# The first half of an input projection by a seven-product scheme, ahead of two attentions

## Chip, cores and metric

One core of one Trainium2 chip runs one layer of an encoder in float32. The metric is device time in microseconds, the median of several runs. In the profile's names, PE is TensorE (matmuls), PEld its weight loads, DVE is VectorE, ACT is ScalarE, POOL is GpSimd and SP is SyncE, which here only issues transfers.

## What is computed

```python
h  = rms_norm(x, norm_mix)                # x: 2048 tokens x 1024 features
z  = h @ w_in                             # 1024 x 4352
q_a, k_a, v_a, q_b, k_b, v_b, g_a, g_b = split(z, [512,128,128,512,512,512,1024,1024])
y_a = windowed_gqa(q_a, k_a, v_a, sink)   # 8 heads of 64, 2 K/V heads, |t-s| <= 128, ALiBi, sink
y_b = neighborhood_attn(q_b, k_b, v_b, rpb)  # 8 heads, 32 x 64 grid, 8 x 16 neighbours, learned bias
merged = sigmoid(g_a + b) * (y_a @ w_proj_a) + sigmoid(g_b + b) * (y_b @ w_proj_b)
x = x + merged @ w_out
x = x + relu(rms_norm(x, norm_mlp) @ w_up)**2 @ w_down
out = rms_norm(x, norm_final)
```

## The kernel before

Every float32 operand of a matmul is split into a high part (rounded) and a low part (the rest), and one product takes three matmuls: high by high, high by low, low by high (`mm3`, lines 187 to 189; `mm3s`, lines 735 to 737). `split_weights` and `split` make the parts: ACT casts, then POOL or DVE subtracts.

The layer runs in stages that follow each other in the program; a scheduler orders the instructions of each engine and may mix neighbouring stages.

1. **Start.** `make_h` loads four token tiles of 128 x 1024, normalises them, turns them with 32 transposes and writes `hT` pages (high and low) for one block of 512 tokens; four blocks in all. K and V of attention A and the first tile of Q (`first`) are projected along with it.
2. **Attention A.** 32 units (`attn_a`: 2 groups of heads x 16 blocks of 128 queries), each with scores, softmax, transposes and PV. Between them stand `dense` pieces: one piece is one tile of 128 columns of `w_in` times one block of 512 tokens, 24 matmuls (`feature_tile`). `paced` lets each piece go only after a given unit is done. There are 40 such pieces in this stage.
3. **V of attention B**, by tokens: `hT` is the stationary operand and 512 columns of weights move, 16 x 24 matmuls. Then the gate columns of token block 0, 16 pieces (`gate_tile`).
4. **Attention B.** 32 units (`attn_b`: 8 heads x 4 column groups), filled with the gate pieces of blocks 1 to 3: 48 pieces, five of them kept for after the last unit. Each head needs three bias tiles (`make_bias_b`: three loads, then POOL adds a mask), in two buffers.
5. **Projections, gates and `w_out`**, then the **up projection** and the **down projection**. Both of these use a scheme of seven block products for a 2 x 2 block product (Strassen's, in Winograd's form): sums of blocks of the weights (`up_left`) and of the tokens (`up_right`) are multiplied, and sums of products give the result (`up_quad`).

Q, K, V and the gates go to DRAM after the projection and are loaded again by the attentions. Buffers come from pools: a load into a buffer waits until the last reader of its tile before is done, and a pool on the left or right side of SBUF can be given up as a whole, whereupon the next pool lies in its place. Loads are issued by SP in order, most stores by ACT (`put`, `flush`).

Of the kernel before, what the change touches and what calls it, by code (L numbers as in the profile page):

```python
# [90 lines left out]
def encoder_layer(ctx, tc, x, norm_mix, w_in, b_gate, sink, rpb, w_pa, w_pb, w_out,  # L91
# [11 lines left out]

    cp = pool("cp", side="left")
    s_w = ExitStack()
    wp = pool("wp", side="right", stack=s_w)
    dp = pool("dp", space=DRAM)
    s_pp = ExitStack()
    pps = {t: pool(f"pp_{t}", space=PSUM, stack=s_pp) for t in ("mm", "s", "pt", "av")}

    n_ps = [0]

# [6 lines left out]
    def T(pl, shape, dt, tag, bufs):  # L119
        n_t[0] += 1  # L120
        return pl.tile(shape, dt, tag=tag, bufs=bufs, name=f"{tag}_{n_t[0]}")
# [23 lines left out]
    qs_a = [dp.tile([2, P, S], F32, name=f"qs_a{t}") for t in range(4)]  # L145
    qs_b = [dp.tile([2, P, S], F32, name=f"qs_b{t}") for t in range(4)]
    ks_a = dp.tile([2, P, S], F32, name="ks_a")
    ks_b = [dp.tile([2, P, S], F32, name=f"ks_b{t}") for t in range(4)]
    vs_a = dp.tile([S, 2, P], F32, name="vs_a")
    vs_b = dp.tile([S, BH, P], F32, name="vs_b")  # L150
# [21 lines left out]
    def slice_of(parts, pl=wp):  # L172

        raw = T(wp, [P, KC, P], F32, "raw", 2)
# [4 lines left out]
        hl = T(pl, [P, 2, KC, P], F32R, "whl", 2 if pl is wp else 1)  # L179
        split_weights(raw, hl)  # L180
        return hl
# [23 lines left out]
    def rstd_of(pl, t):  # L205

        st = T(pl, [P, 4], F32, "st", 4)
        junk = T(pl, [P, 512], F32, "junk", 1)
        for n in range(2):
            A.activation(junk, t[:, n * 512 : (n + 1) * 512], AF.Square, accum_out=st[:, n : n + 1])  # L210
# [5 lines left out]
    def normalised(pl, tiles):  # L216

        for t in tiles:
            V.tensor_scalar(t, t, rstd_of(pl, t), float(D) ** 0.5, ALU.mult, ALU.mult)

    def transposed(tiles, gain, pages, banks):

        hi, lo = pages
        for k in range(KC):
            ps = psum(*banks[k % len(banks)])
            for t in range(4):
                PE.transpose(ps[:, t * P : (t + 1) * P], tiles[t][:, k * P : (k + 1) * P], ident)
            h, l = hi[k // 4][:, k % 4, :], lo[k // 4][:, k % 4, :]
            A.activation(h, ps, AF.Copy, scale=gain[:, k : k + 1])  # L229
            V.scalar_tensor_tensor(out=l, in0=ps, scalar=gain[:, k : k + 1], in1=h.bitcast(F32),  # L230
                                   op0=ALU.mult, op1=ALU.subtract)

    def pages_of(pl, tag, bufs):
        return ([T(pl, [P, 4, BT], F32R, tag, bufs) for _ in range(2)],
                [T(pl, [P, 4, BT], F32R, tag, bufs) for _ in range(2)])


    s_h1 = ExitStack()
    s_h0 = ExitStack()
    s_x = ExitStack()  # L240
    h1 = pool("h1", side="left", stack=s_h1)
    h0 = pool("h0", side="left", stack=s_h0)
    xp = pool("xp", side="left", stack=s_x)
    xf = x[0]
    hp = []

    def make_h(b):
        pg = pages_of(h1 if b else h0, "hT", 12 if b else 4)
        tiles = [load_tile(xp, "xin", 8, xf[b * BT + t * P : b * BT + (t + 1) * P]) for t in range(4)]
        if b == 0:  # L250
            with tc.issue_after(last_dma[0]), nc.allow_non_contiguous_dma(reason="small per-feature vectors"):
                SY.dma_start(g_mix, norm_mix[0].rearrange("(k p) -> p k", p=P))
                SY.dma_start(g_mlp, norm_mlp[0].rearrange("(k p) -> p k", p=P))
                SY.dma_start(bg, b_gate[0].rearrange("(k p) -> p k", p=P))
                SY.dma_start(sink_t, bcast(sink[0], AH))
        normalised(xp, tiles)
        transposed(tiles, g_mix, pg, (("pt", 2), ("s", 2), ("pt", 2), ("s", 2), ("av", 1)))
        hp.append(pg)


    def qk_tile(pl, col, dst, scale, tiled=False, whl=wp):
        hl = slice_of([(cols(w_in[0], col), KC)], whl)
        yield
        for b in range(NB):
            ps = psum("mm", 3)
            feature_tile(ps, hl, hp[b])
            th = T(wp, [P, BT], F32, "z", 2)
            tl = T(pl, [P, BT], F32, "el", 2)
            if tiled:

                pv = ps.rearrange("p (r j c) -> p j r c", r=8, j=4)
                hv, lv, hr, lr = (flipped(t) for t in (th, tl, th.bitcast(F32R), tl.bitcast(F32R)))
                A.copy(hr, pv)
                V.tensor_tensor(out=lr, in0=pv, in1=hv, op=ALU.subtract)
            else:
                A.activation(th.bitcast(F32R), ps, AF.Copy, scale=scale)
                V.scalar_tensor_tensor(out=tl.bitcast(F32R), in0=ps, scalar=scale, in1=th,
                                       op0=ALU.mult, op1=ALU.subtract)
            flush()
            for e in range(2):  # L280
                for z, t in enumerate((th, tl)):
                    put(dst[e, z * 64 : z * 64 + 64, b * BT : (b + 1) * BT], t[e * 64 : e * 64 + 64, :])
            yield

    def v_tile(pl, col, dst):
        hl = slice_of([(cols(w_in[0], col), KC)])
        yield
        for b in range(NB):
# [4 lines left out]
            p2 = psum("mm", 3)  # L293
            for t in range(4):
                PE.transpose(p2[:, t * P : (t + 1) * P], vt[:, t * P : (t + 1) * P], ident)
            flush()
            v2 = T(pl, [P, 4, 2, 2, 64], F32, "v2", 1)
            p2v = p2.rearrange("p (t e d) -> p t e d", t=4, e=2)
            A.copy(v2[:, :, :, 0].bitcast(F32R), p2v)
            V.tensor_tensor(out=v2[:, :, :, 1].bitcast(F32R), in0=p2v, in1=v2[:, :, :, 0], op=ALU.subtract)  # L300
            put(dst[b * BT : (b + 1) * BT].rearrange("(t p) e d -> p t (e d)", p=P),
                v2.rearrange("p t e z d -> p t (e z d)"))
            yield

    make_h(0)
    first = [qk_tile(xp, O_KA, ks_a, 1.0), v_tile(xp, O_VA, vs_a), qk_tile(xp, O_QA, qs_a[0], 0.125, whl=xp)]
    for f in first:
        next(f)
    for b in range(NB):
        if b + 1 < NB:  # L310
            make_h(b + 1)
        for f in first:
            next(f, None)
    for f in first:
        next(f, None)
    flush()
    s_x.close()


    s_a = ExitStack()  # L320
    ap_ = pool("ap", side="left", stack=s_a)
    rp = rpb[0]
    for n, (w, lo_rel) in enumerate(((24, -8), (32, -8), (24, -15))):
        tb = T(ap_, [BH, T_ROWS, w], F32, "v2", 1)
# [11 lines left out]
    def make_bias_a(g):  # L336
        t = T(ap_, [P, 4, 384], F32, "biasa", 1)
# [6 lines left out]
    def attn_a(g, i):  # L344
# [5 lines left out]
        for t in range(2):  # L350
            SY.dma_start(q[:, 2 * t : 2 * t + 2, :].bitcast(F32),
                         qs_a[2 * g + t][:, :, i * P : (i + 1) * P].rearrange("e p t -> p e t"))
        ka = T(ap_, [P, 2, 384], F32R, "ka", 2)
        SY.dma_start(ka[:, 0, lo:hi].bitcast(F32), ks_a[g, :, base + lo : base + hi])
        SY.dma_start(ka[0:64, 1, lo:hi].bitcast(F32), ks_a[g, 64:128, base + lo : base + hi])
        SY.dma_start(ka[64:128, 1, lo:hi].bitcast(F32), ks_a[g, 0:64, base + lo : base + hi])
        v = T(ap_, [P, 3, P], F32R, "va", 3)
        SY.dma_start(v[:, c0:c1, :].bitcast(F32),
                     vs_a[base + lo : base + hi, g, :].rearrange("(c p) d -> p c d", p=P))
# [66 lines left out]
    def units_a(g):  # L426
        make_bias_a(g)
        for i in range(16):
            yield attn_a(g, i)

    for _ in chain([qk_tile(ap_, O_QA + P, qs_a[1], 0.125)]):
        pass
    flush()
    dense = [qk_tile(ap_, O_QA + 2 * P, qs_a[2], 0.125), qk_tile(ap_, O_QA + 3 * P, qs_a[3], 0.125)]
    for t in range(4):
        dense.append(qk_tile(ap_, O_QB + t * P, qs_b[t], 1.0, tiled=True))
        dense.append(qk_tile(ap_, O_KB + t * P, ks_b[t], 0.125))
    fill = chain(dense)
    drive(units_a(0))
    paced(fill, range(8), 40, 0, 3)  # L440
    flush()
    drive(units_a(1))
    last_a = done[-1]
    paced(fill, range(8, 40), 40, 0, 3)
    del done[:]
    flush()
    s_a.close()

# [12 lines left out]
    gates_0 = chain(gate_tile(f, (0,)) for f in range(16))  # L461


    s_v = ExitStack()
    vp = pool("vp", side="left", stack=s_v)
    with tc.issue_after(last_a):
        for _ in range(4):
            next(gates_0)
    hl = T(vp, [P, 2, KC, BT], F32R, "whl", 1)
    for half in range(2):  # L470
        raw = T(vp, [P, 4, BT], F32, "raw", 2)
# [664 lines left out]
```

## Time and profile before

| what | value |
|---|---|
| runs | 2748.17, 2746.87, 2747.84 us, median 2747.84 |
| profiled execution | 2745.41 us, span 2743.6 us, granted TensorE clock 0.990 |
| busy | PE 2672.1 us (97%), DVE 1391.6 (51%), ACT 1181.5 (43%), POOL 808.5 (29%) |
| transfers | 482.73 MB, mean 176 GB/s |

The profile lists for a stretch of time the busy time of each engine with its number of instructions in brackets, then the granted TensorE clock, the share of time in which the 16 DMA engines were busy, and GB/s. In a list of instructions the columns are start, duration, engine and line, operation, tiles written and read, count, and in square brackets the idle time before and what ended it. Lines of a grouped list end in busy time, mean ns of one, and idle time before.

### The profile page before, as it was taken

The numbers are of one execution on the slowest core, as the hardware profiler recorded it, in microseconds if no ns is written. First come the engines' busy times: TensorE is split into PE (matmuls) and PEld (weight loads), VectorE is DVE, ScalarE is ACT, GpSimd is POOL, SyncE is SP. The second block draws the span as 40 slices with busy tenths as digits, with TensorE's granted clock in tenths as the row PEclk, the third lists the DMA queues.
The fourth block names the chain that finished last, engine by engine and source line by source line (L and its number), as shares of the span: only waits on it lengthen the run. The fifth ranks groups of instructions, "written<-read, shape, count | busy, mean of one in ns | idle before, by whom it ended". The sixth has DMA issues, their size and how long they took to land.

```text
span 2743.6 us, 35309 instructions
## 1 busy us (share of the span) xinstructions
PE 2672.1 (97%) x12472; PEld 2217.4 (81%) x12472; DVE 1391.6 (51%) x2174; ACT 1181.5 (43%) x2159; POOL 808.5 (29%) x614
## 2 busy tenths in 40 slices
PE   7999999999899999899999899989999999999998
PEld 6788888887788888787777688878887888888887
DVE  5155564000444443634436666586654644546666
ACT  7145454212454544533433444554444332322444
POOL 2122232213443441532431365556554000000000
PEclk9999999999999999999999999999999999999999
DMA  6556565436787785744645754474444954445555
GB/s 201 150 163 167 165 165 130 147 111 194 199 198 183 196 195 159 219 137 163 221 126 200 272 174 149 154 232 144 145 139 158 344 173 158 141 158 172 179 188 170
DMA packets 387584, 482.73 MB, mean 176 GB/s; under 512 B 32696, under 2 KB 237112, under 8 KB 386256
## 3 DMA queue, kind: packets, MB, share of 16 engines
q1 hardware_dynamic: 332816, 400.76, 47.7%
q10 hardware_dynamic: 54592, 79.72, 9.5%
q8 instruction: 99, 1.62, 0.3%
q14 instruction: 77, 0.63, 0.1%
HBM read 329.31 MB, written 151.06 MB: 175 GB/s over the span
## 4 chain that ended last, share of the span: by engine, by line
PE 84%; DMA 5%; DVE 5%; ACT 2%; issue 2%; POOL 1%; SPq 1%; ACTq 0%; POOLq 0%; DVEq 0%
PE b L735 14%; PE b L736 14%; PE b L737 14%; PE mm L189 9%; PE mm L188 9%; PE mm L187 9%; PE av L582 2%; PE pt L189 2%; DMA z<-zg 2%; PE pt L571 2%; PE pt L188 2%; PE pt L187 2%; PE s L545 2%; DVE ml L682 1%; PE pt L384 1%
## 5 line engine op out<-in xcount | busy, mean ns | idle before, releaser
L187 PE MATMUL mm<-hT,whl 128*128 128x512 f32 x960 | 383.9, 400 | 4.4 <-ACT hT L229 4.4
L188 PE MATMUL mm<-hT,whl 128*128 128x512 f32 x960 | 382.4, 399 | 0.0
L189 PE MATMUL mm<-hT,whl 128*128 128x512 f32 x960 | 380.9, 397 | 0.0
L736 PE MATMUL b<-dwh,dah 128*128 128x512 f32 x896 | 348.6, 389 | 0.0
L737 PE MATMUL b<-dwh,dah 128*128 128x512 f32 x896 | 346.4, 389 | 0.0
L735 PE MATMUL b<-dwh,dah 128*128 128x512 f32 x896 | 339.6, 389 | 2.7 <-ACT dah L731 2.7
L728 POOL TENSOR_TENSOR c<-c,c 128x512 f32<-128x512 f32 x120 | 233.6, 1961 | 229.6 <-issue 160.7
L170 POOL TENSOR_TENSOR whl<-raw,whl 128x1024 fp32r<-128x1024 f32 x80 | 199.6, 2498 | 299.6 <-ACT whl L169 292.6
L731 ACT CAST dah<-da 128x1024 fp32r<-128x1024 f32 (+1 forms) x128 | 120.8, 945 | 357.5 <-PE b L737 235.9
L732 DVE TENSOR_TENSOR dah<-da,dah 128x1024 fp32r<-128x1024 f32 (+1 forms) x128 | 139.3, 1090 | 226.0 <-ACT dah L731 225.9
L735 PE MATMUL b<-bh,whlb 128*128 128x512 f32 x592 | 232.0, 392 | 5.1 <-ACT whlb L731 2.7
L737 PE MATMUL b<-bh,whlb 128*128 128x512 f32 x592 | 231.0, 392 | 2.7 <-DVE whlb L732 2.6
L736 PE MATMUL b<-bh,whlb 128*128 128x512 f32 x592 | 231.4, 391 | 0.0
L187 PEld LDWEIGHTS mm<-hT,whl 128*128 128x128 f32 x960 | 181.5, 189 | 38.6 <-ACT hT L229 4.6
L188 PEld LDWEIGHTS mm<-hT,whl 128*128 128x128 f32 x960 | 181.8, 189 | 34.8
L189 PEld LDWEIGHTS mm<-hT,whl 128*128 128x128 f32 x960 | 181.4, 189 | 35.1
L735 PEld LDWEIGHTS b<-dwh,dah 128*128 128x128 f32 x896 | 168.2, 188 | 38.0 <-ACT dah L731 3.1
L728 DVE TENSOR_TENSOR c<-b,c 128x512 f32<-128x512 f32 x160 | 108.6, 688 | 177.6 <-PE b L737 171.0
L736 PEld LDWEIGHTS b<-dwh,dah 128*128 128x128 f32 x896 | 168.2, 188 | 34.9
L737 PEld LDWEIGHTS b<-dwh,dah 128*128 128x128 f32 x896 | 168.2, 188 | 34.8
L1026 POOL TENSOR_TENSOR st<-st,power 128x1 f32<-128x1 f32 x16 | 13.6, 857 | 614.8 <-DVE st L1025 614.7
L549 DVE CUSTOM_DVE_ANT_0 sb<-s,biasb 128x384 f32<-128x384 f32 (+2 forms) x128 | 70.7, 560 | 194.6 <-PE pt L571 91.7
(202 smaller groups left out, 5579.4 us busy)
## 6 DMA issues: line engine op xcount, KB each, us to landing
at<-c SPq DMA_DIRECT2D x224, 256.0 KB
da<-at SPq DMA_DIRECT2D x96, 512.0 KB
dw<-in_w_down_dram SPq DMA_DIRECT2D x160, 256.0 KB
raw<-in_w_up_dram SPq DMA_DIRECT2D x32, 1024.0 KB
raw<-in_w_in_dram SPq DMA_DIRECT2D x46, 512.0 KB
zg<-z ACTq DMA_DIRECT2D x64, 256.0 KB
z<-zg SPq DMA_DIRECT2D x64, 256.0 KB
xin<-in_x_dram SPq DMA_DIRECT2D x16, 512.0 KB
```

The lines of the kernel that those rows point to most:

```text
L170: G.tensor_tensor(out=hl[:, 1], in0=raw, in1=hl[:, 0].bitcast(F32), op=ALU.subtract)
L187: PE.matmul(ps, lh, rh, start=first, stop=False)
L188: PE.matmul(ps, lh, rl, start=False, stop=False)
L189: PE.matmul(ps, ll, rh, start=False, stop=last)
L545: PE.matmul(ps[:, :n], q[:, z, i, :], kv[:, B_R0[i] : B_R0[i] + B_NR[i], B_C0[j] : B_C0[j] + w], start=z == 0, stop=z == 1)
L549: V.tensor_tensor_reduce(out=si[:, :n], in0=ps[:, :n], in1=bias[:, o : o + n], scale=1.0, scalar=-3.0e38, op0=ALU.add, op1=ALU.max, accum_ ...
L728: eng.tensor_tensor(out=out, in0=a, in1=b, op=op)
L731: A.copy(hi, src)
L732: eng.tensor_tensor(out=lo, in0=src, in1=hi.bitcast(F32), op=ALU.subtract)
L735: PE.matmul(ps, lh, rh, start=first, stop=False, skip_group_check=True)
L736: PE.matmul(ps, lh, rl, start=False, stop=False, skip_group_check=True)
L737: PE.matmul(ps, ll, rh, start=False, stop=last, skip_group_check=True)
```

## The change

Tokens are treated as two halves of 1024.

**First half, ahead of attention A.** Its whole input projection, all 34 column tiles, runs by the seven-product scheme. `QUADS` lists nine quads of columns: a narrow one (K and V of A, 2 x 128 columns) and eight of 2 x 256. The 2 x 2 blocks are 512 features by 512 tokens on the side of the tokens, 512 features by 128 or 256 columns on the side of the weights. `in_left` makes the seven weight operands, `in_quad` the products in the order 1, 2, 5, 6, 7, 4, 3 and their sums, and `in_result` stores them.

```python
QUADS = [(O_KA, P), (O_QA, 256), (O_QB, 256), (O_KB, 256), (O_VB, 256)]
QUADS += [(O_GA + n * BT, 256) for n in range(4)]
...
for n in (1, 2, 5, 6, 7, 4, 3):
    hl, (rh, rl) = lf[n], right[n]
    for a in range(na):
        ...
        for k in range(4):
            mm3s(ps, hl[:, 0, k, at], hl[:, 1, k, at], rh[:, k], rl[:, k], k == 0 and n in (1, 5, 6), k == 3)
```

Products 1 and 2 need block 0 of the tokens alone. They are issued for the first two quads before block 1 is normalised; then the seven token operands are finished from the transposes:

```python
tiles = x_tiles(xp, 1, 5)
...
ws1 = in_weights(*QUADS[1])
quad0 = in_quad(*QUADS[0], lf0, right)
next(quad0)
left1 = in_left(ws1, 256)
lf1 = next(left1)
quad1 = in_quad(*QUADS[1], lf1, right)
next(quad1)
normalised(xp, tiles, Junk())
...
for k in range(KC):
    ps = zbank(*tbanks[k % 6])
    turned(ps, tiles, k)
    kk = k % 4
    if k < 4:
        scaled_less(t1[:, kk], ps, k, right[1][0][:, kk].bitcast(F32))
        scaled(t3[:, kk], ps, k)
        ...
    else:
        h, l = (t[:, kk] for t in right[3])
        scaled(h, ps, k)
        scaled_less(t1[:, kk], ps, k, t1[:, kk])
        scaled_less(t3[:, kk], ps, k, t3[:, kk])
        scaled_less(l, ps, k, h.bitcast(F32))
page_parts(6, t1)
page_parts(7, t3)
...
page_parts(4, t1)
```

(`scaled` is ACT, `scaled_less` DVE, `page_parts` two casts on ACT and two subtractions on DVE of 1024 elements a row.) In quads 4 and 5 the two token blocks of the second half are normalised, transposed and stored in DRAM (`h1d`); during the last quad they are loaded again and split into `hT` pages, which lie where the pages of products 1, 2, 5 and 6 were.

**Second half, beside the attentions.** The plain pieces of blocks 2 and 3 fill both attentions: 36 in A, 32 gate pieces in B, four of them kept for after the last unit. V of attention B is now made by columns and turned with four transposes a piece, as V of A is; its stage of its own and that of the gates of block 0 are gone.

```diff
-drive(units_a(0))
-paced(fill, range(8), 40, 0, 3)
-flush()
-drive(units_a(1))
-last_a = done[-1]
-paced(fill, range(8, 40), 40, 0, 3)
+drive(attn_a(g, i) for g in range(2) for i in range(7))
+paced(fill, range(12), 36, 0, 3)
+flush()
+drive(attn_a(g, i) for g in range(2) for i in range(7, 16))
+paced(fill, range(12, 36), 36, 0, 3)
...
-    bp = pool("bp", side="left", stack=s_b)
+    bp = pools(s_b, "right", ("masks", "kb", "biasb", "qb"), "b")
+    bp.update(pools(s_b, "left", ("vb", "sb", "stb", "phb", "plb", "yb"), "b"))
...
-    fill = chain(gate_tile(f, (1, 2, 3)) for f in range(16))
+    fill = chain(gate_tile(f, (2, 3)) for f in range(16))
...
-    paced(fill, range(48), 48, 5, 4)
+    paced(fill, range(32), 32, 4, 4)
```

The stores of Q, K and V of A are split by halves in DRAM, so that an early unit of A waits only for the half that it reads, and a unit across the middle loads its K and V in two pieces. Stage 5 is unchanged.

More of the change, by code (lines that the diff above doesn't have):

```diff
@@ L214, in rstd_of, with normalised @@
         return r
-    def normalised(pl, tiles):
+    def normalised(pl, tiles, jp=None):
         for t in tiles:
[L219 to L230, printed above, removed]
-                                   op0=ALU.mult, op1=ALU.subtract)
@@ L233, in pages_of @@
[L233 to L258, printed above, removed]
@@ L261, in qk_tile, with turned, add, split @@
-    def qk_tile(pl, col, dst, scale, tiled=False, whl=wp):
-        hl = slice_of([(cols(w_in[0], col), KC)], whl)
+            V.tensor_scalar(t, t, rstd_of(pl, t, jp), float(D) ** 0.5, ALU.mult, ALU.mult)
+    def turned(ps, tiles, k):
+        for t in range(4):
+            PE.transpose(ps[:, t * P : (t + 1) * P], tiles[t][:, k * P : (k + 1) * P], ident)
+    def add(eng, out, a, b, op=ALU.add):
+        eng.tensor_tensor(out=out, in0=a, in1=b, op=op)
+    def split(src, hi, lo, eng):
+        A.copy(hi, src)
+        eng.tensor_tensor(out=lo, in0=src, in1=hi.bitcast(F32), op=ALU.subtract)
@@ new lines, in mm3s, with halves, ring @@
+    def mm3s(ps, lh, ll, rh, rl, first, last):
+        PE.matmul(ps, lh, rh, start=first, stop=False, skip_group_check=True)
+        PE.matmul(ps, lh, rl, start=False, stop=False, skip_group_check=True)
+        PE.matmul(ps, ll, rh, start=False, stop=last, skip_group_check=True)
+    def halves(t):
+        return t[:, 0:2], t[:, 2:4]
+    def ring(stack, tag, shape, dt, bufs, side="right"):
+        pl = pool(f"r_{tag}", side=side, stack=stack)
+        return lambda: T(pl, shape, dt, tag, bufs)
@@ new lines, in encoder_layer, with __missing__, tile, x_tiles @@
+    xp = pools(s_x, "right", ("xin", "st"), "x0")
+    class Junk(dict):
+        def __missing__(self, tag):
+            return self
+        def tile(self, *a, **k):
+            return in_e()
+    def x_tiles(pl, b, bufs):
+        out = []
+        for t in range(4):
+            xt = T(pl, [P, D], F32, "xin", bufs)
+            r = b * BT + t * P
+            last_dma[0] = SY.dma_start(xt, xf[r : r + P]).ins
+            out.append(xt)
+        return out
+    def in_weights(c, w):
+        ws = []
+        for p in range(2):
+            t = kvw() if w == P else in_raw()
+            SY.dma_start(t, w_in[0][p * BT : (p + 1) * BT, c : c + 2 * w].rearrange("(k p) f -> p k f", p=P))
+            ws.append(t)
+        return ws
@@ new lines, in v_parts @@
+    def v_parts(col, b, vt, p2, v2):
+        for t in range(4):
+            PE.transpose(p2[:, t * P : (t + 1) * P], vt[:, t * P : (t + 1) * P], ident)
+        p2v = p2.rearrange("p (t e d) -> p t e d", t=4, e=2)
+        A.copy(v2[:, :, :, 0].bitcast(F32R), p2v)
+        V.tensor_tensor(out=v2[:, :, :, 1].bitcast(F32R), in0=p2v, in1=v2[:, :, :, 0], op=ALU.subtract)
+        if col == O_VA:
+            dst = vs_a[b // 2][b % 2 * BT : (b % 2 + 1) * BT]
+        else:
+            dst = vs_b[(col - O_VB) // P][b * BT : (b + 1) * BT]
+        return dst.rearrange("(t p) e d -> p t (e d)", p=P), v2.rearrange("p t e z d -> p t (e z d)")
@@ new lines, in is_v, with in_result @@
+    def is_v(col):
+        return col == O_VA or O_VB <= col < O_GA
+    def in_result(col, b, src, in_psum):
+        if col < O_VB and col != O_VA:
+            for dst, t in qk_parts(col, b, src, in_e(), in_e()):
+                SY.dma_start(dst, t)
+            return
+        if in_psum:
+            t = in_e()
+            A.copy(t, src)
+            src = t
+        if is_v(col):
+            SY.dma_start(*v_parts(col, b, src, zbank(tpool, 2), in_v2()))
+        else:
+            f = (col - O_GA) // P
+            SY.dma_start(zg[b][0][f // 8, (f % 8) * P : (f % 8 + 1) * P, :], src)
@@ new lines, in scaled, with scaled_less @@
+    def scaled(out, ps, k):
+        A.activation(out, ps, AF.Copy, scale=g_mix[:, k : k + 1])
+    def scaled_less(out, ps, k, t):
+        V.scalar_tensor_tensor(out=out, in0=ps, scalar=g_mix[:, k : k + 1], in1=t, op0=ALU.mult, op1=ALU.subtract)
+    QUADS = [(O_KA, P), (O_QA, 256), (O_QB, 256), (O_KB, 256), (O_VB, 256)]
+    QUADS += [(O_GA + n * BT, 256) for n in range(4)]
+    tiles = x_tiles(xp, 0, 5)
+    with tc.issue_after(last_dma[0]), nc.allow_non_contiguous_dma(reason="small per-feature vectors"):
+        SY.dma_start(g_mix, norm_mix[0].rearrange("(k p) -> p k", p=P))
@@ new lines, in encoder_layer @@
+    xp = pools(s_z, "right", ("xin", "st"), "x2")
+    next(left1)
+    ws = in_weights(*QUADS[2])
+    next(quad1, None)
+    for q in range(2, len(QUADS)):
+        lf = in_left(ws, 256)
+        next(lf)
+        lf = next(lf)
+        if q + 1 < len(QUADS):
+            ws = in_weights(*QUADS[q + 1])
+        if q in (4, 5):
+            b = q - 2
+            tiles = x_tiles(xp, b, 4)
+            normalised(xp, tiles, Junk())
+            for k in range(KC):
+                ps = zbank(tpool, 2)
+                turned(ps, tiles, k)
+                ht = in_e()
+                scaled(ht, ps, k)
+                SY.dma_start(h1d[b - 2][k * P : (k + 1) * P, :], ht)
+        for _ in in_quad(*QUADS[q], lf, right):
+            pass
```

333 lines of the change are left out of this document (211 added, 122 removed).

## The prediction

> **What bounds the kernel now.** I read the page's span and busy times, then its chain, then the engines by stretch, then the order of time on single engines.
>
> ```profile
> span 2743.6 us, 35309 instructions
> ...
> PE 2672.1 (97%) x12472; PEld 2217.4 (81%) x12472; DVE 1391.6 (51%) x2174; ACT 1181.5 (43%) x2159; POOL 808.5 (29%) x614
> ...
> PE 84%; DMA 5%; DVE 5%; ACT 2%; issue 2%; POOL 1%; SPq 1%; ACTq 0%; POOLq 0%; DVEq 0%
> ```
>
> TensorE has work in 97% of the span and carries 84% of the chain, so a matmul less is worth its start-to-start time wherever the queue stays full, and the question is where it does not. By stretch (engine columns: busy us, instructions):
>
> ```profile
> 0.00:20.00 20.00, 7.28 (x28) 5.52 (x29) 6.02 (x12) 12.62 (x27) 7.64 (x14) 0.88 0.87 263
> 300.00:350.00 50.00, 50.00 (x254) 42.22 (x253) 30.52 (x80) 25.66 (x69) 15.61 (x22) 1.00 0.62 171
> 1650.00:1700.00 50.00, 50.00 (x222) 41.40 (x222) 31.04 (x26) 23.44 (x35) 26.08 (x13) 1.00 0.39 137
> ```
>
> The start is starved, attention A (300 to 350) is full with DVE at 61%, and the up projection, which already runs in this seven-product scheme, is full too. Durations of matmuls overlap, so the price is the distance between starts: first and last of 55 consecutive ones with the tokens in `hT`, then first and last of 197 of the up projection, then two transposes.
>
> ```profile
> 1084.41 0.39 PE L187 MATMUL mm<-hT,whl 128*128 128x512 f32 x1
> ...
> 1096.96 0.39 PE L187 MATMUL mm<-page,whl 128*128 128x512 f32 x1
> ```
> ```profile
> 1619.67 0.39 PE L737 MATMUL b<-bh,whla 128*128 128x512 f32 x1
> ...
> 1664.10 0.39 PE L735 MATMUL b<-bh,whlb 128*128 128x512 f32 x1
> ```
> ```profile
> 12.42 0.27 PE L227 MATMUL s<-ident,xin 128*128 128x128 f32 x1
> 12.53 0.27 PE L227 MATMUL pt<-ident,xin 128*128 128x128 f32 x1
> ```
>
> That is 12.55/54 = 0.2324 us, 44.43/196 = 0.2267 us, and 0.11 us a transpose.
>
> **Term 1, the matmuls.** Before, 34 column tiles times 4 token blocks times 24 matmuls are 3264, of which the 384 of `O_VB` have the weights as moving operand; their count and first and last start are
>
> ```profile
> L187 PE MATMUL mm<-whl,hT x128: 389/389/397, 492.3 to 584.5; 128*128 128x512 f32 x128
> 500.00:550.00 50.00, 50.00 (x222) 41.34 (x221) 6.23 (x9) 6.84 (x11) 4.75 (x2) 1.00 0.33 115
> ```
>
> with 222 in 50 us as in the up projection, so 0.2267. After, the first half has one narrow quad and eight wide ones, 84 + 8 x 168 = 1428 instead of 1632, with the operand shapes of the up projection; the second half keeps 1632. Before: 2880 x 0.2324 + 384 x 0.2267 = 756.4 us. After: 1428 x 0.2267 + 1632 x 0.2324 = 703.0. The term is -53.4 us; at 0.2324 throughout it would be 204 x 0.2324 = -47.4, which I keep as the other end.
>
> **Term 2, transposes.** V of attention B no longer comes out by tokens, so its 4 tiles x 4 blocks are each turned by 4 transposes: 64 x 0.11 = +7.0 us. The casts and subtractions that go with them lie beside other matmuls.
>
> **Term 3, the start.** Before, the first 100 us hold these matmuls on `hT` and these transposes (16 more turn V):
>
> ```profile
> 0.00:100.00 100.00, 68.25 (x272) 51.10 (x273) 21.98 (x32) 19.70 (x32) 0.97 0.59 169
> 0.00:100.00 100.00, 19.96 (x128) 16.48 (x128) 0.97 0.59 169
> ```
>
> 272 x 0.2324 + 144 x 0.11 = 79.0, so 21.0 us are lost. After, products 1 and 2 need token block 0 alone, the other five need block 1 and a long run of sums. In the changed program's order on each engine (it is built, not run), SP issues block 0, the narrow weights, one tile of block 1 and the small vectors ahead of the second quad's weights, 5.5 MB in all with them. At the 263 GB/s of the first row above that is 21 us; with the 60 matmuls that then follow (13.6), products 1 and 2 of both quads end at about 35 us. ACT has the eight squares of block 1 behind the last copy of that quad, so block 1's normalisation starts only there. The durations:
>
> ```profile
> 4.58 0.63 ACT L210 ACTIVATE junk<-xin 128x512 f32<-128x512 f32 x1 [2.36 <-DMA xin<-in_x_dram]
> ...
> 5.33 0.63 ACT L210 ACTIVATE junk<-xin 128x512 f32<-128x512 f32 x1
> ```
> ```profile
> L230 DVE SCALAR_TENSOR_TENSOR hT<-pt,g_mix,hT 128x512 fp32r<-128x512 f32 x16 | 11.9, 745 | 11.2 <-ACT hT L229 11.2
> L728 DVE TENSOR_TENSOR c<-c,c 128x512 f32<-128x512 f32 x8 | 5.3, 688 | 0.1
> ```
> ```profile
> 1480.66 1.21 DVE L728 TENSOR_TENSOR S<-raw,raw 128x1024 f32<-128x1024 f32 x1
> 1481.79 1.22 DVE L732 TENSOR_TENSOR bh<-raw,bh 128x1024 fp32r<-128x1024 f32 x1
> ```
>
> Eight squares 0.75 us apart are 6.0, the copy, reduction, scaling and first transposes about 2.6: the sums begin 8.6 us after that point. On DVE then stand, up to the last half of page 4, 16 `scaled_less` from PSUM (16 x 0.745 = 11.9), 8 operations of 512 (5.5), and 18 of 1024 elements, which follow each other 1.13 us apart in the last two rows (20.3): 37.7 us in line. POOL splits weights beside them:
>
> ```profile
> 1662.67 2.28 DVE L732 TENSOR_TENSOR whlb<-raw,whlb 128x1024 fp32r<-128x1024 f32 x1 [1.32 <-ACT whlb L731]
> L732 POOL TENSOR_TENSOR whlb<-raw,whlb 128x1024 fp32r<-128x1024 f32 x21 | 51.7, 2461 | 44.4 <-ACT whlb L731 44.4
> ```
>
> Beside POOL the same operation takes 2.28 us; POOL's two narrow and two wide splits, about 7 us, cost DVE some 3.5. With the second quad's first sum (2.5) TensorE is full about 53 us after that, at 88 us. By then it has had 120 matmuls and 64 transposes, 34.2 us, and has lost 53.8: +32.8 against before (+22 if the weights come 5 us sooner and POOL costs nothing, +42 if they come as much later and each wide operation is slowed).
>
> [...]
>
> **Term 4, the rest of the scheme and the change of stages.** Per wide quad DVE has nine operations of 1024 and eighteen of 512, 22.6 us against 168 x 0.2267 = 38.1 of TensorE, as in the up projection, which runs full. The pages of the second half come back from DRAM during the last quad. I take +3 us (0 to 15).
>
> **Term 5, attention A.** 36 pieces of 24 matmuls instead of 40, over the same 32 units, with 40 transposes for V. DVE at 61% and a full TensorE before leave room: +3 us (0 to 10).
>
> **Term 6, attention B, the doubtful one.** Its filling falls from 48 gate pieces to 32. Stage B by its matmuls on `hT`, and the middle with its score matmuls (8 a unit):
>
> ```profile
> 652.00:1097.00 445.00, 296.54 (x1154) 211.81 (x1152) 0.00 (x0) 0.00 (x0) 0.98 0.77 193
> 750.00:1050.00 300.00, 204.33 (x781) 141.51 (x781) 0.00 (x0) 0.00 (x0) 1.00 0.78 187
> 750.00:1050.00 300.00, 53.84 (x196) 34.41 (x196) 1.00 0.78 187
> ```
>
> In the middle 300 - 781 x 0.2324 = 118.5 us for 24.5 units, 4.84 a unit; the stage is 1152 x 0.2324 + 32 x 4.84 = 422.6, and 22.4 us are lost at its start and end. After: 768 x 0.2324 + 154.9 = 333.4. Masks, K and the first bias now lie beside the weights and can be loaded during A, so I let 10 of the 22.4 stand. But a unit with one piece lasts 10.4 us where it lasted 12.2, the pieces stand in blocks of 21 matmuls, and some five units have none. What an unfilled unit costs, the last units of before show (first PV matmuls of two):
>
> ```profile
> 1053.75 0.39 PE L582 MATMUL av<-phb,vb 128*128 128x256 f32 x1 [0.97 <-DVE yb L590]
> ...
> 1059.65 0.58 PE L582 MATMUL av<-phb,vb 128*128 128x256 f32 x1 [0.49 <-DVE yb L590]
> ```
>
> 5.9 us for the second half of a unit alone; with its scores 8.3, so 3.5 lost: 17 for five, and 0.4 for each of 27 others, 28 in all. The stage comes to 371.4, which is 73.6 less, where the 16 pieces themselves are 89.2: +15.6 us (-10 if the filling still covers everything, +45 for the bias rival).
>
> **The sum.** -53.4 + 7.0 + 32.8 + 3 + 3 + 15.6 = +8.0 us. The profiled execution took 2745.41 us, 1.8 above its span; the sum gives 2753.4 there. The median of the runs is 2.4 above the profiled one, so 2756.
>
> **Rivals.** *The filling suffices (faster).* If the pieces cover both attentions as they do now, the place is stage B, decided at about 10.5 us a unit. Term 6 is then -8, terms 4 and 5 cost 1 and the start, with its weights sooner, 30: -53.4 + 7 + 30 + 1 - 8 = -23, 2725 us. For it: the middle of B shows no lost time, with gaps hidden by as little as 22 matmuls a unit at places. Against: those were spread, the new ones stand in blocks.
>
> *The bias sets the pace of B (slower still).* Last use of one buffer, its reload, the mask on POOL, first use:
>
> ```profile
> 858.92 0.44 DVE L549 CUSTOM_DVE_ANT_0 sb<-s,biasb 128x288 f32<-128x288 f32 x1
> 862.09 3.23 SPq L511 DMA_DIRECT2D biasb<-tab  x3
> 871.37 2.94 POOL L512 TENSOR_TENSOR biasb<-biasb,masks 128x1280 f32<-128x1280 f32 x1 [6.40 <-DMA biasb<-tab]
> 874.86 0.54 DVE L549 CUSTOM_DVE_ANT_0 sb<-s,biasb 128x384 f32<-128x384 f32 x1
> ```
>
> 15.4 us from free to ready, used 0.5 us later, once a head: a shorter unit waits here. If DMA, at 0.78 of its share in the middle, also slows, a unit stays at 12.2 us and stage B at some 400: term 6 +45, 2785 us.
>
> *The scheme's stage is not full (the change does not do what it says).* If its three weight buffers or DVE beside POOL lose 3.5 us a wide quad, 28 in all, instead of 3: 2781 us. Against it stands the up projection's full row with the same ring.
>
> **How the numbers follow.** Chances: forecast 0.46 (2740 to 2772), filling suffices 0.34, bias 0.13, scheme not full 0.07. The range 2716 to 2790 takes in the faster rival with the spread of the start, and both slower ones. About 0.2% (5.5 us) can be told from no change. Of the forecast a little is faster, 0.13 within; the first rival is nearly all faster: 0.36 faster, 0.13 same, 0.51 slower.
>
> **What would show it.** Right: TensorE with some 54 us lost by 90 us and DVE nearly always busy between 45 and 85; matmuls 0.227 apart until about 390 us; 11 us and more a unit in B, with idle times there that DVE or ACT end. Wrong: TensorE full by 70 us, B at 10.4 us a unit, or matmuls of the scheme 0.232 apart.

## The result and the profile after

The changed kernel takes 2825.1 us (median; 2822.5 to 2831.1) against 2747.4 us of the kernel before in the same comparison: 1.029 times as long, 95% interval 1.0269 to 1.0312. The forecast was 2756 us with a range up to 2790. The profiled execution took 2823.88 us. Its page, span, busy times and chain:

```profile
span 2822.2 us, 35453 instructions
...
PE 2677.7 (95%) x12332; PEld 2202.6 (78%) x12332; DVE 1572.2 (56%) x2354; ACT 1237.4 (44%) x2225; POOL 822.0 (29%) x618
...
PE 74%; DMA 10%; DVE 8%; ACT 3%; issue 3%; POOL 1%; SPq 1%; ACTq 0%; POOLq 0%; DVEq 0%
```

There are 140 matmul instructions fewer, yet PE is busy for 5.6 us more, and its share of the chain falls from 84% to 74%; transfers, DVE and issues took it over. PE's timeline has the borders of the stages (start, duration, instruction): last product of the scheme and first score of attention A; first score of attention B; first gate matmul of stage B (768 matmuls on `hT`, its 32 pieces, follow from there); first PV matmul of B's unit 1 and of its unit 29; last gate matmul and first matmul of stage 5.

```profile
400.77 0.39 PE L239 MATMUL zb<-zh,zwhl 128*128 128x512 f32 x1
401.00 0.28 PE L630 MATMUL s<-ka,qa 128*128 128x256 f32 x1
...
728.58 0.60 PE L775 MATMUL s<-kb,qb 128*128 128x288 f32 x3
...
740.85 0.48 PE L191 MATMUL mm<-hT,whl 128*128 128x512 f32 x1
...
767.24 0.28 PE L812 MATMUL av<-phb,vb 96*128 96x256 f32 x1
...
1118.34 0.38 PE L812 MATMUL av<-phb,vb 96*128 96x256 f32 x1
...
1166.79 0.40 PE L193 MATMUL mm<-hT,whl 128*128 128x512 f32 x1
1167.03 0.39 PE L191 MATMUL mm<-page,whl 128*128 128x512 f32 x1
```

Three sums follow. In the kernel before, the prediction counts stage B from its first gate matmul, at 652, 17 us ahead of the first score. The same border lies at 740.9 here: at the first score (728.6) attention A still has a whole piece, transposes and PV to do. Up to this border the forecast had 652 + 8.0 + 73.6 = 733.6, so the scheme, its start and attention A took 7 us more. Stage B lasted 1167.03 - 740.85 = 426.2 us, where 371.4 were forecast: 54.8 too many. From there to the end it is 2822.2 - 1167.0 = 1655.2 us, against 2743.6 - 1097.0 = 1646.6 before: 8.6 more, in stages whose code did not change. 7.2 + 54.8 + 8.6 is the whole miss of 70.6 us in the span.

By stretch (busy us, instructions, granted clock, DMA share, GB/s), first the start and the scheme, then attention A:

```profile
50.00:60.00 10.00, 0.00 (x0) 0.00 (x0) 9.93 (x14) 5.76 (x10) 0.00 (x0) 0.52 0.00 0
60.00:70.00 10.00, 5.29 (x12) 3.88 (x13) 10.00 (x14) 2.91 (x3) 0.00 (x0) 0.50 0.00 0
...
100.00:390.00 290.00, 287.13 (x1312) 237.24 (x1310) 155.74 (x187) 110.69 (x161) 46.12 (x24) 1.00 0.52 162
```
```profile
450.00:500.00 50.00, 50.00 (x259) 42.19 (x258) 33.44 (x90) 30.15 (x75) 17.32 (x23) 1.00 0.68 182
```

DVE works without a pause while TensorE stands, then the scheme and A are full, but for 5 us at A's beginning (401 to 450). The trouble lies between the first PV of units 1 and 29 of stage B. I call this stretch the **middle**: 28 units. It is shown for the kernel after, and then for the kernel before.

```profile
767.20:1118.30 351.10, 306.32 (x1655) 254.36 (x1653) 164.95 (x428) 167.17 (x410) 147.22 (x151) 0.95 0.76 175
```
```profile
694.30:1047.90 353.60, 347.65 (x1965) 303.50 (x1966) 165.67 (x439) 180.90 (x432) 151.94 (x152) 0.99 0.78 188
```

The middle is as long as before, with 310 matmuls and transposes fewer in it. In order of PE's timeline it holds 576 gate matmuls after and 885 before. With the prediction's prices (0.2324 us a gate matmul, 4.84 us of attention a unit) the work in it is 576 x 0.2324 + 28 x 4.84 = 269.4 us after and 341.2 before. So it loses 81.7 us after, and 12.4 before. A unit takes some 12.5 us on average whether it has 32 gate matmuls in it or 21.

Two rows of the waits in stage B (engine and line, waited for; us in total, times, longest) and one place in the timeline of DVE, POOL, ACT and SP show what a unit waits for:

```profile
POOL biasb L742 <- DMA biasb<-tab: 137.7, 19, 13.7
ACT sb L785 <- DVE stb L782: 93.4, 22, 7.9
```
```profile
936.25 0.56 SPq L758 DMA_DIRECT2D qb<-qs_b  x1
...
937.68 0.59 ACT L806 CAST phb<-pt 128x512 fp32r<-128x512 f32 x1
937.69 0.68 DVE L820 TENSOR_TENSOR yb<-av,yb 64x512 f32<-64x512 f32 x1
...
940.46 5.73 SPq L765 DMA_DIRECT2D vb<-vs_b  x4
...
941.22 0.17 DVE L782 TENSOR_SCALAR stb<-stb 128x4 f32<-128x4 f32 x1
...
946.05 2.88 POOL L742 TENSOR_TENSOR biasb<-biasb,masks 128x1280 f32<-128x1280 f32 x1 [10.01 <-DMA biasb<-tab]
947.14 0.53 ACTq L170 DMA_DIRECT2D y_b<-yb  x1
947.77 0.53 ACT L785 ACTIVATE sb<-sb,stb 128x288 f32<-128x288 f32 x1 [9.50 <-DMA qb<-qs_b]
...
948.97 0.56 DVE L779 CUSTOM_DVE_ANT_0 sb<-s,biasb 128x384 f32<-128x384 f32 x1 [7.57 <-POOL biasb L742]
```

Two queues stand still at once. POOL waits 10 us for the bias and DVE, behind it, 7.6 us for POOL: that is the forecast's bias rival. But ACT waits too. The exponentials (L785) have had their maximum since 941.4 and run only at 947.8, because ahead of them in ACT's order stands the issue of the store of `yb`. Its data was there at 938.4, and the issue went out at 947.1. ACT had been free since 938.3, so it stood still for 8.9 us at this issue. In the trace's records the 1856 transfers of this kernel, loads and stores, name eight semaphores, 232 transfers each; the updates of these eight that the records put down to transfers, 28958, are 15.6 for each. The instruction just ahead of this issue in ACT's records waits for the same semaphore that the store then names. The transfer that had named it before was the load of Q which SP had issued at 936.25, as the bracket of ACT's row has it: its last update came at 947.07, and the issue went out 0.08 us later. So an exponential stood behind a load that it does not need. Gaps of over 0.3 us on ACT's timeline that end in its own issue add up to 85 us in the middle after (28 gaps), and to 29 us before. In 26 of the 28 the records have the wait for the store's own semaphore, and in 21 the issue went out within 0.1 us of its last update. In 75 of the 85 us the data to be stored was there; the semaphore's holder before was a load of Q in 50 of these 75 and a load of the bias in 19.

### The profile page after: what moved, and what is told of

Same layout as the page of the kernel before. It is cut to its first block, busy times and chain, and to the rows that moved or that the text cites. A ratio compares the mean times of both kernels' runs of the same rounds, so it can differ in the third digit from the quotient of the medians.

```text
span 2822.2 us, 35453 instructions
## 1 busy us (share of the span) xinstructions
PE 2677.7 (95%) x12332; PEld 2202.6 (78%) x12332; DVE 1572.2 (56%) x2354; ACT 1237.4 (44%) x2225; POOL 822.0 (29%) x618
## 4 chain that ended last, share of the span: by engine, by line
PE 74%; DMA 10%; DVE 8%; ACT 3%; issue 3%; POOL 1%; SPq 1%; ACTq 0%; POOLq 0%; DVEq 0%
PE b L237 14%; PE b L239 14%; PE b L238 14%; PE mm L191 3%; PE mm L193 3%; PE mm L192 3%; PE zb L237 3%; PE zb L238 3%; PE zb L239 3%; DMA biasb<-tab 2%; DMA z<-zg 2%; PE pt L193 2%; PE pt L191 2%; PE pt L192 2%; PE av L812 1%
## 5 line engine op out<-in xcount | busy, mean ns | idle before, releaser
L237 PE MATMUL b<-dwh,dah 128*128 128x512 f32 x896 | 339.6, 389 | 2.1 <-ACT dah L233 2.1
L191 PE MATMUL mm<-hT,whl 128*128 128x512 f32 x544 | 223.2, 410 | 0.0
L192 PE MATMUL mm<-hT,whl 128*128 128x512 f32 x544 | 217.7, 400 | 0.0
L193 PE MATMUL mm<-hT,whl 128*128 128x512 f32 x544 | 216.8, 399 | 0.0
L237 PE MATMUL zb<-zh,zwhl 128*128 128x512 f32 x476 | 189.8, 400 | 26.1 <-ACT zh L233 10.4
L174 POOL TENSOR_TENSOR whl<-raw,whl 128x1024 fp32r<-128x1024 f32 x66 | 160.7, 2435 | 152.1 <-ACT whl L173 138.5
L238 PE MATMUL zb<-zh,zwhl 128*128 128x512 f32 x476 | 188.7, 396 | 0.0
L239 PE MATMUL zb<-zh,zwhl 128*128 128x512 f32 x476 | 185.0, 395 | 0.0
```

The costliest lines, as they stand in the source:

```text
L174: G.tensor_tensor(out=hl[:, 1], in0=raw, in1=hl[:, 0].bitcast(F32), op=ALU.subtract)
L191: PE.matmul(ps, lh, rh, start=first, stop=False)
L192: PE.matmul(ps, lh, rl, start=False, stop=False)
L193: PE.matmul(ps, ll, rh, start=False, stop=last)
L237: PE.matmul(ps, lh, rh, start=first, stop=False, skip_group_check=True)
L238: PE.matmul(ps, lh, rl, start=False, stop=False, skip_group_check=True)
```

## Experiments

P is the theory that the bias's way from free to ready sets a unit's pace; D that the bytes do; F that the blocky filling and the attention's own chain do; Q, formed after the second group, that ACT's issues wait and hold what is behind them. "Middle" is always the 28 units from first PV to first PV; its work is 269.4 us where there are 576 gate matmuls in it.

### Is it the change at all?

The kernel before, with a third of the filling of stage B taken out:

```diff
-    fill = chain(gate_tile(f, (1, 2, 3)) for f in range(16))
+    fill = chain(gate_tile(f, (2, 3)) for f in range(16))
...
-    paced(fill, range(48), 48, 5, 4)
+    paced(fill, range(32), 32, 4, 4)
...
-                SY.dma_start(g, zg[b][0][n, f * P : (f + 1) * P, :])
+                SY.dma_start(g, zg[2 if b == 1 else b][0][n, f * P : (f + 1) * P, :])
```

> The kernel before with 32 gate pieces in attention B instead of 48: the gate columns of token block 1 are left out, and stage 5 reads those of block 2 in their place. This is what the change does to stage B, alone. If stage B were bound by its matmuls, 16 x 24 x 0.2324 = 89 us would go (span 2655). The prediction's term 6 says 74 less (span 2670). Theories P, D and F all say that a unit stays at some 12.3 us, so that only 10 to 25 us go: span 2720 to 2735.

It took 2757.7 us, longer than with the 16 pieces.

```profile
698.50:1049.20 350.70, 311.11 (x1646) 257.00 (x1646) 160.38 (x422) 163.94 (x401) 147.09 (x150) 0.93 0.76 176
```

The middle is that of the changed kernel (350.7 against 351.1, 81.3 lost). Stage 5 begins at 1092.6 instead of 1097.0, so 89 us of matmuls less bring some 4 us. The later stages then take 16.7 us more. The loss in B thus needs neither the scheme nor the new placing of the buffers; the thin filling alone makes it. The theories had 10 to 25 us less, and no loss behind it.

### Bias: bytes or wait?

Without the loads; with three buffers instead of two; and in three tiles, each with its own load and addition:

```diff
-            SY.dma_start(t[:, o : o + n], src)
-        G.tensor_tensor(out=t[...], in0=t[...], in1=masks[...], op=ALU.add)
+        m = masks[:, jstart[jt] : jstart[jt] + jlen[jt]]
+        G.tensor_tensor(out=t[:, : jlen[jt]], in0=m, in1=m, op=ALU.add)
```
```diff
-        t = T(bp, [P, 1280], F32, "biasb", 2)
+        t = T(bp, [P, 1280], F32, "biasb", 3)
```
```diff
+            t[IT[i]] = T(bp, [P, (384, 512, 384)[IT[i]]], F32, f"biasb{IT[i]}", 2)
+            SY.dma_start(t[IT[i]][:, :n], src)
+            G.tensor_tensor(out=t[IT[i]][:, :n], in0=t[IT[i]][:, :n], in1=masks[...], op=ALU.add)
```

> Changed kernel without the loads of the bias of attention B: the POOL addition stays, with its two buffers and its place, but adds the masks to themselves, so the relative bias is left out of the scores of attention B. In the changed kernel the middle units of stage B stand 12.5 us apart with 24 gate matmuls each, where their matmuls alone are 10.4. Theory P (a bias buffer's way from free to ready, and what POOL holds behind it, sets the pace): the 28 middle units come down towards 10.4 to 11 us, stage B from 439 to 380 to 395 us, span 2765 to 2780. Theory D (the transfers are saturated): the same sign, since a fifth of the bytes of a unit goes, 2765 to 2790. Theory F (blocky filling and the attention's own chain of DVE and ACT): pace and span stay, 2815 to 2825.

> Changed kernel with three bias buffers instead of two: the same bytes, the same additions on POOL, but a load may start a buffer's life earlier. Theory P: most of the lost 2.1 us a unit goes, stage B 380 to 400 us, span 2765 to 2785. Theory D: the bytes are the same, 2815 to 2825. Theory F: the same, 2815 to 2825.

> Changed kernel with the bias of a unit in three tiles of its own (384, 512, 384 columns, two buffers each, the same memory) instead of one tile of 1280: each part comes free after its own last use, has its own load and its own, shorter, addition. Theory P: the way from free to ready falls from some 15 us to 9 or 10, half or more of the 59 us goes, span 2765 to 2795. Theories D and F: 2815 to 2825.

2788.7, 2814.3 and 2809.0 us; middles of 313.7, 337.1 and 333.4. Without loads:

```profile
764.10:1077.80 313.70, 293.87 (x1653) 245.34 (x1651) 160.31 (x427) 165.84 (x408) 136.92 (x150) 0.98 0.61 159
```

37 of the 82 us hang on the loads. The buffers alone give only 14 and 18, much less than P said, and the time without loads lies in D's range alone. 44 us stay without any bias load: more than this F cannot have. To part bytes from wait, the loads were put back for nobody: into a buffer that is never read, and then once more with a small DVE reading at each unit's end that holds the loads to their place.

```diff
+        x = T(bp, [P, 1280], F32, "biasx", 1)
...
+            SY.dma_start(x[:, o : o + n], src)
...
+        if j != 2:
+            V.tensor_scalar(mx[:, 0:1], x[:, 0:1], -1.0, None, ALU.mult)
```

> Changed kernel in which the bias of attention B is loaded as before, byte for byte, but into a buffer that nobody reads; POOL adds the masks to themselves, as in the run without the loads (the relative bias is left out of the scores). Against that run it puts the traffic back, and not the wait. Theory P (the way of a buffer from free to ready): the time of the run without loads, 2789 us, within 6. Theory D (the bytes): the time of the changed kernel, 2815 to 2825. Both in part: between, and the share is read from it.

> As the earlier run with unread bias loads, but with one small reading on DVE at the end of each unit, which holds each load to its place in stage B (in the earlier run all of them had gone out during attention A). POOL adds the masks to themselves and waits for no load. Q: ACT's waits at its store issues come back with the loads, middle 330 to 350, span 2805 to 2822. P: the middle stays at 309 to 314, span 2785 to 2795. D: as Q, but with ACT idle ahead of other instructions than its store issues.

The first, without the reading, was no test of what it was meant for. With nobody to wait for them the scheduler sent the loads out during attention A. B's middle fell to 308.7 us, but the kernel took 2854.8: in A, which had been full, SP's queue waited 70 us for these loads, and TensorE idled (a row of A's waits of SP, and a stretch of A):

```profile
SPq L742 <- DMA biasx<-tab: 70.4, 24, 6.2
```
```profile
500.00:550.00 50.00, 42.21 (x185) 33.64 (x186) 23.44 (x64) 22.52 (x58) 13.39 (x18) 0.91 0.75 186
```

The second, in place, took 2825.9, 4 us above Q's range, with a middle of 339.6, inside it:

```profile
778.00:1117.60 339.60, 305.44 (x1646) 253.93 (x1644) 162.13 (x442) 162.87 (x400) 134.42 (x149) 0.95 0.80 181
```

No addition waits for a bias load there, and still 26 of the 37 us are back; ACT's gaps at its own issues are back too, 83 us against 17 without the loads. By this order of taking things away, the wait of POOL is worth the other 12. What is left is D or Q.

### ACT's issues

The same kernel, and the changed kernel itself, with the stores of stage B issued by SP:

```diff
-            A.dma_start(*pending.pop(0))
+            store[0].dma_start(*pending.pop(0))
-            A.dma_start(zg[b][0][f // 8, ...], z)
+            store[0].dma_start(zg[b][0][f // 8, ...], z)
+    store[0] = SY          # stage B only
     s_b = ExitStack()
```

> The run with the bias loads unread but in place, and the stores of stage B on SP besides: no engine waits for a bias load, and ACT issues no transfer. The loads in place cost 26 us of the middle against the run without loads (340 against 314), with ACT idle 83 us ahead of its own store issues. Theory Q (an issue on ACT waits for an earlier transfer and holds ACT): the middle comes back to 305 to 318, span 2780 to 2795. Theory D (the bytes): it stays at 335 to 345, span 2815 to 2825.

> Changed kernel whose stores of attention B's outputs and of the gates during stage B are issued on SP's queue, not on ACT's. A new theory Q stands behind it: in the 351 us of the 28 middle units ACT sat idle 85 us directly ahead of its own store issues, with the data long there (29 us in the kernel before, 17 without the bias loads), so the issue itself waits for earlier transfers, and the exponentials of the next unit stand behind it on ACT. Q: most of that goes, the middle falls to 315 to 330 us, span 2785 to 2802. Theory P (POOL waits for the bias): ACT is idle for the same time ahead of other instructions, span 2815 to 2825.

With the unread loads: 2787.3 us, as Q said.

```profile
774.10:1085.80 311.70, 290.30 (x1645) 245.82 (x1644) 156.39 (x442) 163.71 (x400) 134.60 (x149) 0.98 0.91 198
```

The same bytes now move at 198 GB/s with the DMA engines 0.91 busy, and the middle is that of the run without loads (311.7 against 313.7). So D is out, and Q is shown for these 26 to 28 us. In the changed kernel alone, however, the move brought 5.6 us (2819.5; middle 344.3): Q's forecast for it failed. ACT's gaps at its own issues are gone there, but its idle time in the middle falls only from 183.9 us to 178.6. POOL still waits for the bias, and ACT, with DVE, stands behind that (two rows of the waits of its middle):

```profile
POOL biasb L744 <- DMA biasb<-tab: 127.6, 16, 13.1
ACT sb L787 <- DVE stb L784: 114.6, 23, 7.8
```

### Blocks of filling, and the steps together

Pieces handed out in halves of 12 matmuls, with a mark after half a unit:

```diff
+                if k == 3:
+                    yield
...
+            if pair % 2:
+                done.append(last)
...
+    for n in range(64):
+        at = n * 64 // 56 - 8 if n < 56 else 63
```

> Changed kernel whose 32 gate pieces of attention B are handed out in 64 halves of 12 matmuls, each after a half of a unit (two marks a unit instead of one). Same instructions, same bytes. Theory F (one block of 21 matmuls a unit leaves the rest of the unit bare): of the 28 us that the middle units still lose without the bias loads, 15 to 20 go, in this run perhaps less, since the bias still waits: 2795 to 2815. Theories P and D: 2820 to 2826.

> Changed kernel with the halves of the run before and the bias in three tiles of its own with three buffers each. If wait and blocks add, the loss of 66 us in the middle of stage B falls to 15 to 25: 2770 to 2785. If traffic sets the pace (D), no more than the best of the single steps: about 2805.

> The stores on SP together with the half pieces and the bias in three tiles with three buffers. Q: the last of the stalls at each head's border go, units of 10.3 to 10.6 us throughout, middle 300 to 310, span 2770 to 2782. If the stalls at the heads' borders are the loads themselves (P or D), 2790 to 2797 as without the stores moved.

2807.2, 2796.9 and 2781.9 us. The middle (with 588 gate matmuls, 272.2 us of work) loses 62.9, 49.0 and 31.2: the halves take 19 us away, the bias in three tiles of three buffers 14 more, the stores on SP 18 more. The last one:

```profile
772.60:1076.00 303.40, 288.97 (x1658) 249.80 (x1656) 154.90 (x421) 167.83 (x402) 153.66 (x189) 0.96 0.87 199
```

Most of its units follow each other in 10.2 to 10.7 us, the 10.4 that the prediction had for a unit with one piece; what remains sits near the borders of heads (13 to 16 us there). The second of the three missed its range, 2770 to 2785: ACT's gaps at its own issues add up to 81 us there.

### The start, the end, and the kernel before

```diff
+    normalised(xp, tiles, Junk())
     quad0 = in_quad(*QUADS[0], lf0, right)
...
     next(quad1)
-    normalised(xp, tiles, Junk())
```

> Changed kernel with the squares and the normalisation of token block 1 issued ahead of the first products' copies, not behind them. Term 3 of the prediction puts the squares only behind the last copy of the second quad: if so, the sums begin 8 to 10 us sooner, TensorE is full at about 79 us instead of 88, span 2812 to 2815. If the weights or DVE's line set the start, nothing moves (2820 to 2824).

2818.3 us, between the two expectations. DVE's first `scaled_less` of block 1, in the changed kernel and here:

```profile
45.74 2.73 DVE L432 SCALAR_TENSOR_TENSOR zraw<-zb,g_mix,zh 128x512 f32<-128x512 f32 x4 [1.02 <-PE zb L227]
```
```profile
33.15 2.73 DVE L432 SCALAR_TENSOR_TENSOR zraw<-zb,g_mix,zh 128x512 f32<-128x512 f32 x4 [1.70 <-PE zb L227]
```

12.6 us sooner, and by 100 us TensorE has lost 43.6 instead of 54.2 (214 and 167 matmuls x 0.2267 and 72 transposes x 0.11, taken from 100). So the place of the squares was what term 3 said. Stage 5 begins 12.0 us sooner, at 1155.0, after a middle of the same length (351.0). Only 5.7 us arrive at the end, since the stages from there on, whose code is the same, take 6.3 us more.

> Changed kernel with half pieces, the bias in three tiles with three buffers, the stores of stage B on SP, and the squares of token block 1 first. If the steps add (2782 and 5.5 less): 2774 to 2779, still 28 to 36 us above the kernel before, since the start loses some 20 us more and stage B saves some 50 of the 89 us of its pieces.

> The four steps, with one gate piece left for after the last unit instead of four: the halves are spread over nearly all units. If the bare units and the stage's end lose what their matmuls do not fill (11 us at the end, 3 a bare half unit): 2762 to 2772. If the left pieces covered the loads of stage 5's first pages, the time goes over to the start of stage 5: 2774 to 2782.

The four steps add: 2774.1 us, 1.0125 of the kernel before (1.0108 to 1.0142). That is 51 us off the changed kernel, and 32 short of the one before. Spreading the pieces to the end (`62` for `56` in the line above) failed with 2790.0, where I had offered 2782 as the worst. Stage 5 began 3 us sooner (1107.5 against 1110.7), and from there on everything took 20.3 us more. Its first 30 us in this run, and in the one of the four steps:

```profile
1107.50:1137.50 30.00, 17.89 (x48) 11.49 (x47) 17.04 (x17) 17.16 (x22) 2.45 (x1) 0.72 0.70 240
```
```profile
1110.70:1140.70 30.00, 25.70 (x108) 19.62 (x107) 23.33 (x18) 17.98 (x22) 15.77 (x7) 1.00 0.90 298
```

60 matmuls fewer get done, with TensorE waiting for the weights and pages that ACT, POOL and DVE make (its longest idle time there, 4.04 us, ends in ACT's `page`). So the time went over to the start of stage 5, as the second of the two expectations had it, and more of it.

> The kernel before with the same stores on SP's queue during stage B. Its middle units are full of matmuls and lose 12 us in all, and ACT waits 29 us at its issues there. Q: 0 to 12 us less (2735 to 2747); if the thicker filling hides ACT's waits altogether, no change.

> The kernel before with its bias of attention B in three tiles of two buffers each. Theory P holds there only where the filling is thin: its middle units lose 13 us in all: 0 to 8 us less (2736 to 2744), a version that would beat both by a little; if the thick filling covers the wait altogether, no change.

Two of the steps in the kernel before: stores on SP 1.0031 (1.0019 to 1.0042), a little slower, which neither expectation had; bias in three tiles 0.9996 (0.9986 to 1.0005), no change. What costs a thinly filled stage tens of us costs next to nothing where 32 matmuls a unit cover it. No version beats the kernel before.

## Why the prediction was wrong

- **Terms 1, 2, 4 and 5** held within their ranges. The scheme's stage is full (287.1 of 290 us) and ended at 401; its matmuls start 0.227 us apart. Attention A lasted 740.9 - 401.0 = 339.9 with 5 us of idle time, nearly all in its first 49. Together with term 3 they were to put the first gate matmul of B at 733.6, and it came 7 us later. The rival of a scheme that is not full fell, and so did "the filling suffices".
- **Term 3**, the start: 53.8 us lost by about 88 was forecast, 54.2 was found. Products 1 and 2 of both quads end at 36.0 (35), and the line of DVE was as long as counted: 37.7 us, from 45.7 to 83.4. The 5.5 MB are counted in units of 2^20 bytes; at the 263 GB/s they make 21.9 us, not 21, a slip of 1 us. The granted clock was 0.52 and 0.50 in the two rows of the start above, and from 66.07 to 70.34 the scheme's matmuls started 0.427 us apart, for 0.227 where it was 1.00. The sum had no term for this; what it cost is part of the 54.2.
- **Term 6** failed: 426.2 us for 371.4. The prediction had 269.4 us of work and 28 of thin filling for the middle, 297.4 in all. It took 351.1, which is 53.7 of the 54.8. Ahead of the middle and behind it, 26.4 and 48.7 us make 75.1 for the 74.0 forecast: the 10 us that I let stand there were about right.
- **The step in it that was wrong** is the price of a thinly filled unit. I took it from the last, bare units, 8.3 us, where no bias is reloaded, no gate is stored and nothing stands behind the queues. The 118.5 us that I read from the middle of the kernel before are the attention's matmul time; that it fitted so well only said that 32 matmuls a unit cover the waits, not that 24 would. The kernel before with 32 pieces shows it without the rest of the change: its middle loses 81.3 us, where the prediction had 28 for the whole stage.
- **The rival of the bias** gave the pace (12.2 us a unit; 12.5 came), and too short a stage, 400: 32 units at its pace and 10 us. With the ends as they were (75.1 us) its 28 middle units would have made 417. The way that it read, from free to ready, is 15.0 us from the end of the last use (15.4 counts from its start). Its mechanism is the smaller part. By the runs, in the order in which things were taken away, of the 82 us of the middle some 12 are POOL's wait for the bias, 26 are ACT's issues that wait for transfers, and 44 are left with no bias loads at all. Taken away alone, ACT's issues bring 7, so the shares are not separate costs. The halves, tried with the loads in place, took 19 away, so about that much lies with the blocks of filling; how the rest divides between the borders of heads and the attention's own chain stays open.
- **The chances**: with 0.13 on the bias rival I had the right place at a low chance, and no mechanism in which two queues stall side by side. That the kernel would be slower had 0.51.
- **The signs**: all that were named for "right" came (54 us lost, DVE busy 39.2 of 40 us between 45 and 85, 0.227, over 11 us a unit). "11 us and more a unit" has no upper end, so it could not tell the forecast from the bias rival.
- **Not in the prediction at all**: 8.6 us in the unchanged later stages. 6.5 of them come before the last matmul of `w_out` (389.1 us after the start of stage 5, for 382.6). The thin filling in the kernel before brought 16.7 there, so the scheme is not needed for it. From stage 5 on the same instructions took 1643.5 to 1680.8 us in the runs here; what orders them so is open.

## What to carry over

A stage that looks bound by TensorE at 98% may have several other floors just below it. Before work is taken out of it, count what a unit would take without the filling in the middle of the stage, with its loads, stores and in-order queues, not at its bare end. A store issued by a computing engine can be a wait for that engine, and not only for the data: here ACT stood still for 75 us of the middle at stores whose data was there, nearly all of it for loads that had named the store's semaphore before. Look at the gaps that end in the engine's own issues. And where two waits cover each other, removing either one shows little, and only the removal of both tells their price: here the stores on SP brought 5.6 us alone, and 38.6 where no addition waited for the bias.

## What was not expected of the chip

- The granted clock was 0.95 over the middle of the changed kernel, whose idle times are scattered and at most 6.2 us each, and 0.99 in the middle before. In the records of the clock it is 1.00 there but for nine stretches of 3.4 us (one of 6.8) at 0.50. In the 3.4 us ahead of each, TensorE had been idle for 1.6 us or more in all; ahead of the one shown here, no single idle time was longer than 1.3 us:

```profile
859.00:862.70 3.70, 1.81 (x7) 0.79 (x5) 1.39 (x4) 3.30 (x10) 0.82 (x1) 1.00 0.51 126
862.70:866.10 3.40, 3.34 (x15) 3.29 (x16) 1.25 (x4) 2.80 (x6) 3.12 (x5) 0.50 0.63 194
```

TensorE had work in 32 us of these stretches. In two of them gate matmuls follow each other, 0.427 us apart (from 891.56 to 893.27, and from 1092.52 to 1094.65) where they were 0.233 apart at 1.00 (866.19 to 867.82). If all the work in the 32 us was slowed as much, that is an estimated 15 of the 82 us that the middle loses: part of the price of its waits.
- The DMA engines at 0.91 of the time and 198 GB/s did not slow the units (11.1 us each); at 0.76 and 175 GB/s a unit took 12.5. A high share of transfers was no sign of what bounds here.
